# Seven products in place of eight in a feed-forward network's first down block, on one Trainium2 core

## The chip, the cores and the metric

The kernel runs on one core of a Trainium2 chip. The time is in device microseconds (us) of one execution. A core has TensorE (matrix products; the profile calls it PE, and its weight loads PEld), VectorE (DVE), ScalarE (ACT), GpSimd (POOL), SyncE (SP, which here only issues DMA transfers) and 16 DMA engines. Each engine works through its own instructions in order and waits on semaphores for the others.

## The reference

One layer of a causal decoder with 256 positions of 1024 channels in float32: attention of two kinds with a gated merge, then a gated feed-forward network with a causal convolution of width 3, then a last norm. The change lies in the feed-forward network:

```python
def conv_ffn(h, w_up, conv_w, conv_b, w_down):
    u, gate = jnp.split(h @ w_up, 2, axis=-1)          # each 256 x 2816
    up = jnp.pad(u, ((0, 0), (CONV_WIDTH - 1, 0), (0, 0)))
    uc = conv_b
    for j in range(CONV_WIDTH):
        uc = uc + conv_w[j] * up[:, j:j + S]
    return (jax.nn.gelu(uc) * gate) @ w_down           # 2816 x 1024
...
x = x + conv_ffn(rmsnorm(x, g_ffn[l]), w_up[l], conv_w[l], conv_b[l], w_down[l])
return rmsnorm(x, g_final)
```

## The kernel before

Every float32 operand of a matrix product is split in two parts that TensorE takes at its faster float32r rate: a high part (a copy rounded to float32r) and a low part (the value less the high part). A product is then three: high x high, high x low and low x high. For the weights, ScalarE makes the high part (`split_hi`, L131, tile whi) and VectorE the low one (`split_lo`, L135, tile wlo).

The weights come in units of 128 x 2048 numbers (1 MB), each loaded by one DMA transfer on SP's queue into one of three `raw` buffers; whi and wlo have three buffers each, too. The list `units` is walked in order, and the loop body writes out by hand what each engine does around a unit: at the start of a step the low part of the next unit (`lo_of(i + 1)`) and the load five units ahead, then the unit's products, then the high part of the unit two ahead (`hi_of(i + 2)`), then the evacuation. A raw buffer is free for the load three units later once both parts are made.

The feed-forward network goes in 11 blocks of 256 of the 2816 hidden channels. Block j has an up unit u_j, a gate unit g_j and a down unit d_j, and a down unit comes two blocks late: the order is u0 g0 u1 g1 u2 g2 d0 u3 g3 d1 u4 g4 d2 and so on. NFIRST is the number of u0 in the list, so that units NFIRST + 4, 5, 7 and 8 are u2, g2, u3 and g3. After u_j VectorE scales the result (U, L599), ScalarE and VectorE convolve it (C, L603, L611); after g_j ScalarE applies the gelu (L617), and VectorE multiplies (M, L624). M is then split like a weight: ah on ScalarE (L634) and al on VectorE (L643, `post_g`, issued a unit later).

A down unit multiplies M (two halves t of the positions by two halves kt of the channels) with 256 x 1024 weights. One half of the output columns takes the plain form (`mm_down_part`, L662). For the other half, blocks 1 to 8 use a form of the 2 x 2 block product with seven products instead of eight (`mm_sums`, L676): it needs sums of the four pieces of M (L629, L631, L632, which widen ah and al from 512 to 1024 columns) and of the four pieces of the weights (`split_sums`: W, L172 to L174, and its parts Wh, L176, and Wl, L178). Block 0 and the last two use the plain form for both halves. With the three products of each split, a down unit in the plain form is 48 products of 128 x 256, one with the seven-product form 24 + 21 = 45. `FIRST_SUM = 1` is the first block of that form.

Of the kernel before, what the change touches and what calls it, by code (L numbers as in the profile page):

```python
# [11 lines left out]
F32 = mybir.dt.float32  # L12
F32R = mybir.dt.float32r
# [14 lines left out]
SHARED = {25: 1024, 26: 1024}  # L28
ORDER = np.arange(D).reshape(8, 4, 32).transpose(1, 0, 2).reshape(-1)
QUARTERS = ((0, 0, 512), (1, 0, 512), (0, 512, 256), (1, 512, 256), (1, 768, 256), (0, 768, 256))  # L30
FIRST_SUM = 1
EPS = 1e-6
BIG = 1e30
UW = 2240
# [62 lines left out]
def build(ctx, tc, a, out):  # L97
# [35 lines left out]
    def split_lo(u, c0=0, c1=None, eng=None):  # L133
        c1 = c1 or u.n
        (eng or V).tensor_sub(u.lo[:, u.o + c0:u.o + c1], u.raw[:, c0:c1], u.hi.bitcast(F32)[:, u.o + c0:u.o + c1])  # L135

    def split_range(u, c0, c1):
        split_hi(u, c0, c1)
        split_lo(u, c0, c1)

    def hi_of(i):
        if 2 <= i < len(units):
            if units[i].load is not None or units[i] is downs[NF - 1] and units[i].hi is not None:
                return
            split_tiles(units[i])
            split_hi(units[i], 0, 1792 if units[i] in downs[FIRST_SUM:NF - 2] else None)

    def lo_of(i):
        if 2 <= i < len(units):
            if i == 27:  # L150
                split_lo(units[i], 1024, 2048, P)
                return
            if i in SHARED:
                split_lo(units[i], 0, SHARED[i])
                split_lo(units[i], SHARED[i], 2048, P)
                return
            if i == NFIRST + 1:
                split_lo(units[i], 0, 1024)
                split_lo(units[i], 1024, 2048)
                return  # L160
            if units[i] in downs[FIRST_SUM:]:
                return
            if units[i].load is None:
                split_lo(units[i])
# [424 lines left out]
        units.append(Unit(2048, mm_out(c), ev_out(c)))  # L589


    ffn = {}

    def ev_u(j):
        def f(u):
# [24 lines left out]
    def ev_g(j):  # L620
        def f(u):
            f_ = ffn["pool"]
            M = f_.tile([128, 8, 128], F32, name="M", tag="M", bufs=2)
            V.tensor_tensor(out=M[:, 0:4].rearrange("p (c t) s -> p c (t s)", c=2), in0=u.p, in1=ffn["C", j],  # L624
                            op=OP.mult)
            n = 4
            if FIRST_SUM <= j < NF - 2:
                n = 8
                V.tensor_tensor(out=M[:, 4:6], in0=M[:, 0:4:3], in1=M[:, 1, None].to_broadcast([128, 2, 128]),  # L629
                                op=OP.subtract)  # L630
                V.tensor_tensor(out=M[:, 6], in0=M[:, 5], in1=M[:, 0], op=OP.add)  # L631
                V.tensor_sub(M[:, 7], M[:, 2], M[:, 6])  # L632
            h = f_.tile([128, 8, 128], F32R, name="ah", tag="ah", bufs=4)
            A.activation(h[:, :n], M[:, :n], AF.Copy)  # L634
            ffn["M", j] = M[:, :n], h
        return f

    def post_g(j):
        def f():
            M, h = ffn["M", j]  # L640
            n = M.shape[1]
            l = ffn["pool"].tile([128, 8, 128], F32R, name="al", tag="al", bufs=4)
            V.tensor_sub(l[:, :n], M, h.bitcast(F32)[:, :n])  # L643
            ffn["a", j] = (h, l)
        return f
# [22 lines left out]
    def mm_sums(u, j):  # L668

        wh, wl = [w[:, u.o + 1024:u.o + 1792].rearrange("p (b c) -> p b c", b=3) for w in (u.hi, u.lo)]  # L670
        sh, sl = [w.rearrange("p (b c) -> p b c", b=4) for w in (u.wh, u.wl)]
        h, l = ffn["a", j]
        for q, x, k in ((2, 2, 1), (1, 0, 0), (3, 7, 2), (6, 6, 6), (5, 5, 4), (7, 4, 5), (4, 3, 7)):
            yh, yl = (wh[:, k], wl[:, k]) if k < 4 else (sh[:, k - 4], sl[:, k - 4])
            for n, (w, a_) in enumerate(((yh, h), (yh, l), (yl, h))):
                T.matmul(ffn["P"][q], a_[:, x], w, start=j == FIRST_SUM and n == 0 and q in (1, 5),  # L676
                         stop=j == NF - 3 and n == 2 and q in (1, 5, 6, 7), skip_group_check=True)

    def mm_down(j):
# [534 lines left out]
            nc.sync.dma_start(X[32 * j:32 * j + 32, :, b * 256:b * 256 + 256],  # L1214
                              Y[32 * b:32 * b + 32, :, j * 256:j * 256 + 256])

    post = []
    for i, u in enumerate(units):
        if i == FIRST_ITEM:
            rt["identr"] = att.tile([128, 128], F32R, name="identr")  # L1220
            A.activation(rt["identr"], ident, AF.Copy)
        if i == 9:
            cmp_sum()
        for it in batches.get(i - 1, []):
            it.fin()
        if i == FIRST_ITEM + 6:
            dil_tiles()
        for it in at(i):
            if isinstance(it, Dil):
                it.split()  # L1230
        for it in at(i - 3):
            it.te()
        if i == 11:
            cmp_kv_ev()
        for it in at(i - 1):
            it.sm()
        if i > 2 and i != 6:
            lo_of(i + 1)
        if i == 10:
            cmp_gelu()  # L1240
        for it in at(i - 1):
            it.sm2()
        for it in at(i - 1):
            it.send("MA" if isinstance(it, Cmp) else {20: "KH", 21: "KL"}.get(i, "MB%d" % (i % 2)))
        if u in downs[3:7]:
            spread(downs.index(u) - 3)
        load_to(i + LA)
        if i == 14:
            nc.sync.dma_start(xT, a["xT"])
        if i == 3:  # L1250
            hi_of(5)
            mixer_tiles()
            u1.evac(u1)
        if i == 4:
            split_keys()
        if i == 14:

            ob = att.tile([128, 4, S], F32R, name="ob", tag="qa")
            OB.update(h=ob[:, 0:2], l=ob[:, 2:4])
        if i in (23, 24):  # L1260
            for c in range(2):
                m = ML[i - 23, c]
                A.activation(m, m, AF.Sigmoid)
        if i == NFIRST:
            st.close()
            ffn["pool"] = ctx.enter_context(tc.tile_pool(name="ffn", bufs=1))
            gf = ffn["pool"].tile([128, D], F32, name="gf")
            nc.scalar.dma_start(gf, bass.AP(tensor=a["g_final"].tensor, offset=a["g_final"].offset,
                                            ap=[[0, 128], [1, D]]))
            X = ffn["pool"].tile([128, 2, D], F32, name="X")  # L1270
            sq = ffn["pool"].tile([128, 512], F32, name="sq")
            Y = ffn["pool"].tile([128, 2, D], F32, name="Y")
        if 24 <= i <= 25:
            hi_of(i + 2)
        if i in (3, 24, NFIRST + 2):
            rt["kick"] = "own"
        u.mm(u)
        if i == 2:
            split_tiles(units[3])
            for c in (0, 1024):  # L1280
                split_hi(units[3], c, c + 1024)
        if not 24 <= i <= 26 and i > 1 and i != 3:
            hi_of(i + 2)
        if i == 5:
            lo_of(7)
        if units[min(i + 2, len(units) - 1)] in downs[FIRST_SUM:NF - 2]:
            split_sums(units[i + 2])
        if units[min(i + 2, len(units) - 1)] is downs[NF - 2]:
            split_lo(units[i + 2])
        if i == 2:  # L1290
            lo_of(3)
            row_scale()
            u0.evac(u0)
            ev_cmp2()
        if i == NFIRST + 1:
            rt["R2"] = rows_of(rt["rs2"], "R2", "o")
            units[NFIRST].evac(units[NFIRST])
        if post:
            post.pop()()
        if u.pre:  # L1300
            u.pre(u)
        if i + 3 == len(units) - 1:
            hi_of(i + 3)
        if u.evac and i not in (0, 1, NFIRST):
            u.evac(u)
        if i + 3 == len(units) - 1:
            split_lo(units[i + 3])
        if i == 4:
            tables_pool4()
        if i in (6, 7):  # L1310
            q_parts(i - 6)
        if i == 7:
            gates_of()
        if u in downs[2:6]:
            turn(downs.index(u) - 2)
        if u.pre:
            post.append(post_g(len([q for q in units[:i] if q.pre])))
        first = [it for it in at(i) if isinstance(it, Nsa) or isinstance(it, Dil) and it.t]
        for it in first:
            it.qk()  # L1320
        if i == 11:
            at(i)[-1].by_keys()
        for it in at(i - 2):
            it.tr()
        for it in at(i):
            if it not in first:
                it.qk()
        for it in batches.get(i, []):
            it.pv()
        if i == 9:  # L1330
            cmp_fold()
        if i == 10:
            cmp_kv()
# [79 lines left out]
```

## Time and profile before

| what | value |
|---|---|
| median of 3 runs | 384.53 us (383.98 to 384.89) |
| the profiled execution: its time | 384.13 us |
| its span, first to last instruction | 382.2 us |
| granted TensorE clock, mean | 0.998 |
| busy: TensorE, VectorE, ScalarE, GpSimd | 374.9, 313.4, 225.1, 34.9 us |

The span is what the trace covers; some 1.9 us of the execution lie around it. A busy share is an average over stages. In rows of the timeline the first number is the start in us from the span's start, the second the length in us, then engine, line, operation, output <- inputs with shapes, and, in brackets, idle time of that engine just before and what ended it. The chain is followed back from the last instruction: each step to what released it, or to the instruction before it on its engine.

### The profile page before, as it was taken

Reading aid. Unit: us, or ns where it says so; the run is one execution under the profiler, and the core shown is the slowest. Engines: PE = TensorE matmul, PEld = TensorE weight load, DVE = VectorE, ACT = ScalarE, POOL = GpSimd, SP = SyncE. Lnnn points to the kernel's source line nnn. Section 1 sums busy time; section 2 is a strip of 40 time slices with the busy share of each in tenths; the row PEclk is TensorE's granted clock in tenths of the full one; section 3 lists DMA queues with packets and bytes.
Section 4 is the critical chain, followed back from the end, with each engine's and each line's share of the span. In section 5 each row is a group of like instructions: output and inputs, shape, how many; then the busy total and the mean of one; then the engine's idle time right before and its main releaser. Section 6 shows DMA issues by size and latency. Waiting matters only on the chain.

```text
span 382.2 us, 8160 instructions
## 1 busy us (share of the span) xinstructions
PE 374.9 (98%) x3393; PEld 369.3 (97%) x3393; DVE 313.4 (82%) x541; ACT 225.1 (59%) x315; POOL 34.9 (9%) x62
## 2 busy tenths in 40 slices
PE   8999999999999999999999999999999999999993
PEld 6999999999999999999999999999999999999993
DVE  5959699994996876468887799997998989889874
ACT  5966636875985745745634756554574455745613
POOL 4011400001000000250333000000000000000011
PEclk9999999999999999999999999999999999999999
DMA  8999354468454656463547355845658476585002
GB/s 274 423 391 345 138 218 168 166 237 332 172 201 150 233 222 224 151 220 101 202 149 290 126 211 199 322 146 187 219 177 294 148 239 229 156 304 202 21 0 110
DMA packets 14996, 79.30 MB, mean 207 GB/s; under 512 B 1776, under 2 KB 3312, under 8 KB 7280
## 3 DMA queue, kind: packets, MB, share of 16 engines
q1 hardware_dynamic: 14528, 77.94, 56.3%
q10 hardware_dynamic: 432, 0.85, 0.7%
q8 instruction: 26, 0.43, 0.4%
q14 instruction: 10, 0.08, 0.1%
HBM read 71.05 MB, written 1.05 MB: 189 GB/s over the span
## 4 chain that ended last, share of the span: by engine, by line
PE 96%; DMA 1%; DVE 0%; ACT 0%; issue 0%; SPq 0%; POOLq 0%; POOL 0%; ACTq 0%
PE ps_d L206 36%; PE ps_d L211 18%; PE ps_o L206 5%; PE ps_s L662 5%; PE ps_t L662 4%; PE ps_d L309 3%; PE ps_o L676 3%; PE ps_o L211 3%; PE ps_d L366 2%; PE ps_t L206 2%; PE ps_t L909 2%; DMA first<-in_first_dram 1%; PE ps_o L978 1%; PE ps_t L676 1%; PE ps_o L564 1%; PE ps_o L1099 1%
## 5 line engine op out<-in xcount | busy, mean ns | idle before, releaser
L135 DVE TENSOR_TENSOR wlo<-raw,whi 128x2048 fp32r<-128x2048 f32 (+3 forms) x62 | 132.5, 2140 | 4.5 <-ACT whi L131 4.5
L206 PE MATMUL ps_d<-hTh,whi 128*128 128x256 f32 x512 | 119.0, 278 | 0.0
L206 PE MATMUL ps_d<-hTl,whi 128*128 128x256 f32 x512 | 117.9, 276 | 0.0
L131 ACT ACTIVATE whi<-raw 128x2048 fp32r<-128x2048 f32 (+3 forms) x62 | 112.7, 1828 | 7.3 <-DMA raw<-in_wts_dram 3.1
L206 PEld LDWEIGHTS ps_d<-hTh,whi 128*128 128x128 f32 x512 | 96.1, 188 | 0.9 <-issue 0.7
L206 PEld LDWEIGHTS ps_d<-hTl,whi 128*128 128x128 f32 x512 | 96.1, 188 | 0.0
L211 PE MATMUL ps_d<-hTh,wlo 128*128 128x256 f32 x512 | 63.3, 276 | 0.0
L211 PEld LDWEIGHTS ps_d<-hTh,wlo 128*128 128x128 f32 x512 | 60.5, 188 | 0.0
L634 ACT ACTIVATE ah<-M 128x1024 fp32r<-128x1024 f32 (+1 forms) x11 | 10.4, 946 | 23.1 <-DVE M L632 19.9
L603 ACT ACTIVATE C<-U,small 128x256 f32<-128x256 f32 x22 | 12.0, 595 | 17.7 <-DVE U L599 17.7
L176 ACT ACTIVATE Wh<-W 128x1024 fp32r<-128x1024 f32 x8 | 8.5, 1064 | 22.4 <-DVE W L174 22.4
L611 DVE SCALAR_TENSOR_TENSOR C<-U,small,C 128x256 f32<-128x256 f32 x44 | 18.6, 480 | 2.1 <-ACT C L603 2.1
L946 ACT ACTIVATE E<-E,ast 128x256 f32<-128x256 f32 (+1 forms) x32 | 14.1, 450 | 9.6 <-DVE ast L941 7.7
L1357 POOL TENSOR_TENSOR tiny<-cst,tiny 128x1 f32<-128x1 f32 x2 | 0.5, 228 | 163.0 <-ACT sq L1356 163.0
L624 DVE TENSOR_TENSOR M<-ps_d,C 128x512 f32<-128x512 f32 x10 | 6.9, 690 | 10.0 <-PE ps_d L211 8.5
L135 POOL TENSOR_TENSOR wlo<-raw,whi 128x1024 fp32r<-128x1024 f32 x3 | 7.8, 2598 | 71.3 <-ACT whi L131 71.3
L643 DVE TENSOR_TENSOR al<-M,ah 128x1024 fp32r<-128x1024 f32 (+1 forms) x11 | 11.8, 1072 | 0.0
L206 PE MATMUL ps_d<-whi,hTh 128*128 128x256 f32 x48 | 11.3, 282 | 0.0
L206 PE MATMUL ps_d<-whi,hTl 128*128 128x256 f32 x48 | 11.1, 277 | 0.0
L206 PE MATMUL ps_o<-mixh,whi 128*128 128x256 f32 x48 | 11.0, 276 | 0.0
L206 PE MATMUL ps_o<-mixl,whi 128*128 128x256 f32 x48 | 11.0, 276 | 0.0
L381 DVE TENSOR_TENSOR ML<-ps_d,R 128x512 f32<-128x512 f32 x8 | 5.5, 690 | 6.3 <-PE ps_d L211 6.3
(314 smaller groups left out, 787.2 us busy)
## 6 DMA issues: line engine op xcount, KB each, us to landing
raw<-in_wts_dram SPq DMA_DIRECT2D x59, 1024.0 KB, 5.1
Er<-E SPq DMA_DIRECT2D x6, 512.0 KB, 3.2
first<-in_first_dram SPq DMA_DIRECT2D x7, 384.0 KB, 6.6
Er<-E SPq DMA_DIRECT2D x6, 384.0 KB, 2.9
raw<-in_wts_dram SPq DMA_DIRECT2D x2, 560.0 KB, 8.7
xn<-in_xn_dram SPq DMA_DIRECT2D x2, 512.0 KB, 8.9
w1k<-in_wts_dram SPq DMA_DIRECT2D x2, 512.0 KB, 7.8
w1v<-in_wts_dram SPq DMA_DIRECT2D x2, 512.0 KB, 7.6
```

The source lines that it names most:

```text
L131: A.activation(u.hi[:, u.o + c0:u.o + c1], u.raw[:, c0:c1], AF.Copy)
L135: (eng or V).tensor_sub(u.lo[:, u.o + c0:u.o + c1], u.raw[:, c0:c1], u.hi.bitcast(F32)[:, u.o + c0:u.o + c1])
L206: T.matmul(po, l, r, start=start and bank not in banks, stop=False, skip_group_check=True)
L211: T.matmul(po, l, r, start=False, stop=stop and n == len(ks) - 1, skip_group_check=True)
L309: T.matmul(u.p[:, i], l[:, kt, i * 128:i * 128 + 128], r[:, kt], start=kt == 0 and i == 0 and q == 0, stop=kt == 7 and q == 2, skip_group_ ...
L603: A.activation(C[:, c], U[:, c, 2:], AF.Identity, scale=CW(2, t), bias=CB[:, t:t + 1])
L611: V.scalar_tensor_tensor(C[:, c], U[:, c, w:w + S], CW(w, t), C[:, c], op0=OP.mult, op1=OP.add)
L634: A.activation(h[:, :n], M[:, :n], AF.Copy)
L643: V.tensor_sub(l[:, :n], M, h.bitcast(F32)[:, :n])
L662: T.matmul(ffn["y"][t][ch][:, b:b + 256] if own is None else own, x[:, 2 * kt + t], quarter(w, kt, ch, b), start=j == (0 if own is None el ...
L676: T.matmul(ffn["P"][q], a_[:, x], w, start=j == FIRST_SUM and n == 0 and q in (1, 5), stop=j == NF - 3 and n == 2 and q in (1, 5, 6, 7), s ...
L946: A.activation(self.E[:, i], self.E[:, i], AF.Exp, bias=mn[:, i:i + 1], scale=-1.0, accum_out=dn[:, i:i + 1])
```

## The change

Three things change. First, block 0's down unit takes the seven-product form, too (FIRST_SUM is 0). Second, the sums of M and the making of ah, now in a function `sums`, come later for the first blocks: those of block 0 after g1, of block 1 after g2, of block 2 after d0; from block 3 on they stand after their own g unit as before. Third, for u2, g2, u3 and g3 the second half of the low part (columns 1024 to 2048) is no longer made by VectorE: ScalarE writes the negated, rounded raw weights into it, and a DMA transfer from GpSimd's queue adds the raw weights to it in place.

```diff
-FIRST_SUM = 1
+FIRST_SUM = 0
+NEXT, LATE = {0: (), 1: (0,), 2: (1,)}, (2,)
+ADDED = (4, 5, 7, 8)
...
+    def negate_and_add(u, c0, c1):
+        lo = u.lo[:, u.o + c0:u.o + c1]
+        A.activation(lo, u.raw[:, c0:c1], AF.Copy, scale=-1.0)
+        P.dma_start(out=lo.bitcast(F32), in_=u.raw[:, c0:c1], accum_op=OP.add)
...
             split_hi(units[i], 0, 1792 if units[i] in downs[FIRST_SUM:NF - 2] else None)
+            if i - NFIRST in ADDED:
+                negate_and_add(units[i], 1024, 2048)
...
+            if i - NFIRST in ADDED:
+                split_lo(units[i], 0, 1024)
+                return
...
-            n = 4
-            if FIRST_SUM <= j < NF - 2:
-                n = 8
...
-            h = f_.tile([128, 8, 128], F32R, name="ah", tag="ah", bufs=4)
-            A.activation(h[:, :n], M[:, :n], AF.Copy)
-            ffn["M", j] = M[:, :n], h
+            for k in NEXT.get(j, (j,)):
+                sums(k)
...
+    def sums(j):
+        M, n = ffn["M", j], 4
+        if j < NF - 2:
+            n = 8
...
+        h = ffn["pool"].tile([128, 8, 128], F32R, name="ah", tag="ah", bufs=4)
+        A.activation(h[:, :n], M[:, :n], AF.Copy)
+        ffn["a", j] = h, None
+        post.append(post_g(j, M[:, :n], h))
...
-                T.matmul(ffn["P"][q], a_[:, x], w, start=j == FIRST_SUM and n == 0 and q in (1, 5),
+                T.matmul(ffn["P"][q], a_[:, x], w, start=j == 0 and n == 0 and q in (1, 2, 4, 5),
...
-        if u.pre:
-            post.append(post_g(len([q for q in units[:i] if q.pre])))
+        if u is downs[0]:
+            for k in LATE:
+                sums(k)
```

The order of the instructions shows where this lands. Names in the rows: whi and wlo are the weights' parts, C, M, U, W, ah and al as above. On ScalarE, from the gelu of block 0 to that of block 1 and what follows, before:

```order
L617 ACTIVATE C<-C 128x512 [waits DVE_49]
L634 ACTIVATE ah<-M 128x512 [waits DVE_49]
L131 ACTIVATE whi<-raw 128x2048 [waits DMAHW7_49,PE_49,Activation_49]
L603 ACTIVATE C<-U,small 128x256 [waits DVE_49]
L603 ACTIVATE C<-U,small 128x256
L131 ACTIVATE whi<-raw 128x2048 [waits DMAHW0_49,PE_49,Activation_49]
L617 ACTIVATE C<-C 128x512 [waits DVE_49]
L634 ACTIVATE ah<-M 128x1024 [waits DVE_49]
```

And after, at the same place:

```order
L629 ACTIVATE C<-C 128x512 [waits DVE_49]
L133 ACTIVATE whi<-raw 128x2048 [waits DMAHW7_49,PE_49,Activation_49]
L141 ACTIVATE wlo<-raw 128x1024 [waits PE_49]
L615 ACTIVATE C<-U,small 128x256 [waits DVE_49]
L615 ACTIVATE C<-U,small 128x256
L133 ACTIVATE whi<-raw 128x2048 [waits DMAHW0_49,PE_49,Activation_49]
L141 ACTIVATE wlo<-raw 128x1024 [waits PE_49]
L629 ACTIVATE C<-C 128x512 [waits DVE_49]
L652 ACTIVATE ah<-M 128x1024 [waits DVE_49]
```

The narrow ah of block 0 is gone from its place (the last row is now block 0's wide one, one block later), and a negated copy stands behind each high part, ahead of the next gelu.

On VectorE, from the low part of u2 (unit NFIRST + 4) to U of block 2, before:

```order
L135 TENSOR_TENSOR wlo<-raw,whi 128x2048 [waits DMAHW7_49]
L624 TENSOR_TENSOR M<-ps_o,C 128x512 [waits PE_49,Activation_49]
L629 TENSOR_TENSOR M<-M 128x256 [waits DVE_49]
L631 TENSOR_TENSOR M<-M 128x128 [waits DVE_49]
L632 TENSOR_TENSOR M<-M 128x128 [waits DVE_49]
L135 TENSOR_TENSOR wlo<-raw,whi 128x2048 [waits DMAHW0_49]
L643 TENSOR_TENSOR al<-M,ah 128x1024 [waits Activation_49]
```

And after:

```order
L137 TENSOR_TENSOR wlo<-raw,whi 128x1024 [waits DMAHW7_49]
L637 TENSOR_TENSOR M<-ps_o,C 128x512 [waits PE_49,Activation_49]
L647 TENSOR_TENSOR M<-M 128x256
L649 TENSOR_TENSOR M<-M 128x128 [waits DVE_49]
L650 TENSOR_TENSOR M<-M 128x128 [waits DVE_49]
L137 TENSOR_TENSOR wlo<-raw,whi 128x1024 [waits DMAHW0_49]
L184 TENSOR_TENSOR W<-raw 128x512 [waits DMAHW1_49]
L185 TENSOR_TENSOR W<-W,raw 128x256 [waits DVE_49]
L186 TENSOR_TENSOR W<-W,raw 128x256 [waits DVE_49]
L137 TENSOR_TENSOR wlo<-raw,whi 128x1792 [waits Activation_49]
L660 TENSOR_TENSOR al<-M,ah 128x1024
```

The low parts of u2 and g2 are half as long, the sums after M are block 0's instead of block 1's, and d0's weight sums and low part now stand here, ahead of al.

On GpSimd (POOL), after the norm's last step (L244, now L256), where before nothing came until the kernel's end:

```order
L256 TENSOR_TENSOR tiny<-tiny,cst 128x2 [waits Activation_49]
L142 DMA wlo<-raw 128x1024 [waits DMAHW7_49,DVE_49,Activation_49]
L142 DMA wlo<-raw 128x1024 [waits DMAHW0_49,DVE_49,Activation_49]
L142 DMA wlo<-raw 128x1024 [waits DMASW0_49,DMAHW2_49,DVE_49,Activation_49]
L142 DMA wlo<-raw 128x1024 [waits DMASW1_49,DMAHW3_49,DVE_49,Activation_49]
L1374 TENSOR_TENSOR tiny<-cst,tiny 128x1 [waits Activation_49]
```

The four accumulating transfers are new on this queue; each waits for ScalarE's negated copy. In u2, g2, u3 and g3 the fifth low-part product on TensorE waits for the transfer, the first one for VectorE as before.

More of the change, by code (lines that the diff above doesn't have):

```diff
@@ L589, in build @@
         units.append(Unit(2048, mm_out(c), ev_out(c)))
-    ffn = {}
+    ffn, post = {}, []
     def ev_u(j):
@@ L623, in f, with post_g @@
             M = f_.tile([128, 8, 128], F32, name="M", tag="M", bufs=2)
+            ffn["M", j] = M
             V.tensor_tensor(out=M[:, 0:4].rearrange("p (c t) s -> p c (t s)", c=2), in0=u.p, in1=ffn["C", j],
                             op=OP.mult)
-            n = 4
-            if FIRST_SUM <= j < NF - 2:
-                n = 8
[L629 to L632, printed above, removed]
-            h = f_.tile([128, 8, 128], F32R, name="ah", tag="ah", bufs=4)
-            A.activation(h[:, :n], M[:, :n], AF.Copy)
-            ffn["M", j] = M[:, :n], h
-        return f
-    def post_g(j):
+            for k in NEXT.get(j, (j,)):
+                sums(k)
+        return f
+    def sums(j):
+        M, n = ffn["M", j], 4
+        if j < NF - 2:
+            n = 8
+            V.tensor_tensor(out=M[:, 4:6], in0=M[:, 0:4:3], in1=M[:, 1, None].to_broadcast([128, 2, 128]),
+                            op=OP.subtract)
+            V.tensor_tensor(out=M[:, 6], in0=M[:, 5], in1=M[:, 0], op=OP.add)
+            V.tensor_sub(M[:, 7], M[:, 2], M[:, 6])
+        h = ffn["pool"].tile([128, 8, 128], F32R, name="ah", tag="ah", bufs=4)
+        A.activation(h[:, :n], M[:, :n], AF.Copy)
+        ffn["a", j] = h, None
+        post.append(post_g(j, M[:, :n], h))
+    def post_g(j, M, h):
         def f():
-            M, h = ffn["M", j]
             n = M.shape[1]
@@ L1215, in spread @@
                               Y[32 * b:32 * b + 32, :, j * 256:j * 256 + 256])
-    post = []
     for i, u in enumerate(units):
```

## The prediction

> **What bounds the kernel now.** I read the page's busy times first, then the chain that ended last, then the chain, the ScalarE rows and the VectorE rows of 205 to 255 us, where the changed instructions stand, and last the DMA issues.
>
> ```profile
> PE 374.9 (98%) x3393; PEld 369.3 (97%) x3393; DVE 313.4 (82%) x541; ACT 225.1 (59%) x315; POOL 34.9 (9%) x62
> PE 96%; DMA 1%; DVE 0%; ACT 0%; issue 0%; SPq 0%; POOLq 0%; POOL 0%; ACTq 0%
> ```
>
> TensorE is busy for 374.9 of 382.2 us and holds 96% of the chain: what another engine does counts only once it makes TensorE wait. The chain around the first down product, in order of time (start, length, what):
>
> ```profile
> 221.09 3.63 PE ps_d L206 x32
> ...
> 226.53 3.63 PE ps_d L206 x32
> ...
> 230.15 1.81 PE ps_d L211 x16
> 231.97 0.23 PE ps_s L662 x2
> ...
> 237.18 0.23 PE ps_s L662 x2
> 237.41 3.63 PE ps_d L206 x32
> ...
> 242.85 3.63 PE ps_d L206 x32
> 246.47 1.81 PE ps_d L211 x16
> 248.29 0.45 PE ps_s L662 x4
> ...
> 252.03 1.02 PE ps_o L676 x9
> 253.05 0.34 PE ps_s L676 x3
> 253.39 0.68 PE ps_d L206 x6
> ```
>
> Each piece starts where the last ended, so TensorE has no gap here. d0 (48 products) runs from 231.97 to 237.41, 5.44 us; d1 (24 products of L662 and 21 of L676) from 248.29 to 253.39, 5.10 us. u2, g2, u3 and g3 start at 221.09, 226.53, 237.41 and 242.85; each multiplies the high part for 3.63 us (L206) and the low part for 1.81 us (L211).
>
> **The change part by part.** *The seven products in d0.* d0 becomes what d1 is: 45 products for 48, so 5.44 - 5.10 = 0.34 us less on the path. Everything after d0 starts 0.34 us sooner if nothing is late. This is the only term that shortens the chain; the rest has to stay hidden.
>
> *What ScalarE does for it.* Its rows before:
>
> ```profile
> 213.75 0.63 ACT L617 ACTIVATE C<-C 128x512 f32<-128x512 f32 x1
> 215.14 0.63 ACT L634 ACTIVATE ah<-M 128x512 fp32r<-128x512 f32 x1 [0.76 <-DVE M L624]
> 215.68 1.91 ACT L131 ACTIVATE whi<-raw 128x2048 fp32r<-128x2048 f32 x1
> 218.55 1.10 ACT L603 ACTIVATE C<-U,small 128x256 f32<-128x256 f32 x2 [0.97 <-DVE U L599]
> 219.55 1.91 ACT L131 ACTIVATE whi<-raw 128x2048 fp32r<-128x2048 f32 x1
> 221.36 0.62 ACT L617 ACTIVATE C<-C 128x512 f32<-128x512 f32 x1
> ...
> 238.36 1.71 ACT L131 ACTIVATE whi<-raw 128x1792 fp32r<-128x1792 f32 x1 [0.22 <-DMA raw<-in_wts_dram]
> ...
> 242.34 1.07 ACT L176 ACTIVATE Wh<-W 128x1024 fp32r<-128x1024 f32 x1 [2.27 <-DVE W L174]
> ```
>
> Added: four negated copies of 128x1024 (1.07 each by the Wh row), a Wh for d0 (1.07), and ah of block 0 at 1024 for 512 (0.43 more); d0's high part is 0.20 shorter. Together 5.6 us on an engine that is 59% busy by the page. *What VectorE does.* Its rows before:
>
> ```profile
> 215.02 2.28 DVE L135 TENSOR_TENSOR wlo<-raw,whi 128x2048 fp32r<-128x2048 f32 x1
> 217.22 0.68 DVE L643 TENSOR_TENSOR al<-M,ah 128x512 fp32r<-128x512 f32 x1
> 217.83 0.68 DVE L599 TENSOR_TENSOR U<-ps_o,R 128x512 f32<-128x512 f32 x1
> ...
> 223.08 0.69 DVE L624 TENSOR_TENSOR M<-ps_o,C 128x512 f32<-128x512 f32 x1
> 223.80 0.42 DVE L629 TENSOR_TENSOR M<-M 128x256 f32<-128x256 f32 x1
> ...
> 224.79 2.29 DVE L135 TENSOR_TENSOR wlo<-raw,whi 128x2048 fp32r<-128x2048 f32 x1
> ...
> 240.70 0.68 DVE L172 TENSOR_TENSOR W<-raw 128x512 f32<-128x512 f32 x1
> ...
> 242.22 2.02 DVE L135 TENSOR_TENSOR wlo<-raw,whi 128x1792 fp32r<-128x1792 f32 x1
> 244.17 0.68 DVE L599 TENSOR_TENSOR U<-ps_d,R 128x512 f32<-128x512 f32 x1
> ...
> 245.90 1.67 DVE L611 SCALAR_TENSOR_TENSOR C<-U,small,C 128x256 f32<-128x256 f32 x4
> ...
> 252.32 1.22 DVE L643 TENSOR_TENSOR al<-M,ah 128x1024 fp32r<-128x1024 f32 x1
> 253.45 2.28 DVE L135 TENSOR_TENSOR wlo<-raw,whi 128x2048 fp32r<-128x2048 f32 x1
> ```
>
> Start to start, a low part takes 2.20 us (215.02 to 217.22), one of 1024 takes 1.13 (252.32 to 253.45), the three W sums 1.52 (240.70 to 242.22), the d low part 1.95 (242.22 to 244.17) and the three M sums 0.99 (223.80 to 224.79). Added for d0: W sums 1.52, Wl 1.13, M sums of block 0 0.99, a longer al 0.52, less 0.25 for the shorter low part: 3.9. Removed: four times 2.20 - 1.13 = 4.3. VectorE's total barely falls (0.4 us); what changes is the order.
>
> *Who is late next.* I laid the new order out by hand with these lengths, from 214.38, where the row at 213.75 ends. The high part of u2 no longer waits behind ah: it ends at 216.2, its negated copy at 217.2. U of block 1 starts at 217.2 (no al ahead), C ends on ScalarE at 218.9, then the high part of g2 (220.7) and its negated copy (221.7). Only then comes the gelu (222.3), so M of block 1 ends at 223.0 (before 223.8), M sums of block 0 at 224.0, ah at 225.1, d0's high part at 226.7, d0's low part 228.7, al of block 0 229.9, U of block 2 230.5, its C on ScalarE 231.5, the high part of u3 233.3, its negated copy 234.3, gelu 234.9, M and the sums of block 1 236.7, ah 237.7, the high part of g3 239.5, its negated copy 240.5.
>
> TensorE asks for al of block 0 after 8 products of d0, at 231.97 + 0.91 = 232.9, where it is 3.0 us old. The halves that VectorE still makes are done by 221.5, 225.3, 237.9 and 241.1, wanted (3.63 us into each unit; u3 and g3 0.34 earlier) at 224.7, 230.2, 240.7 and 246.1. Later, the low part of u4 ends at 254.4 and is wanted at 253.39 - 0.34 + 3.63 = 256.7: 2.3 us, the narrowest of VectorE's own.
>
> *The accumulating transfers.* The fifth product of the low part waits for them, 4 x 0.113 = 0.45 us later than the first. From the end of the negated copy to that product there are 225.2 - 217.2 = 8.0 us for u2, 230.6 - 221.7 = 8.9 for g2, 241.2 - 234.3 = 6.9 for u3 and 246.6 - 240.5 = 6.1 for g3. No accumulating transfer is in this trace. The nearest rows (KB each, median us from issue to landing):
>
> ```profile
> raw<-in_wts_dram SPq DMA_DIRECT2D x59, 1024.0 KB, 5.1
> Er<-E SPq DMA_DIRECT2D x6, 512.0 KB, 3.2
> ...
> xn<-in_xn_dram SPq DMA_DIRECT2D x2, 512.0 KB, 8.9
> ```
>
> Low end: 3.2 us, the same 512 KB from SBUF to SBUF. High end: 8.9, the same size queued behind other loads. I take 5.1: the transfer reads its 512 KB and also the 512 KB it adds to, the bytes of one weight load. At 5.1 nothing waits; g3's lands 1.0 us early. The wait of TensorE would be about D - 6.1 for a landing time of D: 2.8 us at 8.9, so the sum lies between -0.34 and +2.5 us. Issuing them costs POOL alone, whose queue holds nothing else here. Nor does the held raw buffer matter at 5.1: u4's weights reuse u3's buffer, freed at 239.4 in place of 237.4, and land 5.1 later at 244.5, when ScalarE wants them at 247.9; g4's follow on SP's queue from 245.6 to 250.7, wanted at 253.1.
>
> Sum: -0.34 us against the profiled execution's 384.13 (span 382.2 and 1.9 around it), so 383.8 there. That execution lies 0.40 under the median of the runs, 384.53; for the median I forecast 384.2. A measurement of this kernel can tell about 0.2%, 0.77 us, from no change, so this counts as the same.
>
> **The rivals.** *The transfers land late (slower).* Place: the fifth low-part product of g3, then of u3. It costs the whole gain at D = 6.1 + 0.34 = 6.4 and +0.77 at 7.2; at 8.0 it gives 384.5 + 1.6 = 386.1. For it: the loads of raw, 5.1 us each, run all through, and g3's transfer is issued (240.5) while u4's load (239.4 to 244.5) runs. Against: the Er row's 3.2.
>
> *VectorE keeps POOL from issuing (slower).* Two rows show the two engines in each other's way:
>
> ```profile
> L135 POOL TENSOR_TENSOR wlo<-raw,whi 128x1024 fp32r<-128x1024 f32 x3 | 7.8, 2598 | 71.3 <-ACT whi L131 71.3
> L231 DVE SCALAR_TENSOR_TENSOR hTl<-xT,small,hTh x8: 473/850/1516, 184.3 to 201.0; 128x256 fp32r<-128x256 f32 x8
> ```
>
> The second runs from 473 to 1516 ns; the slow ones stand beside POOL's sums of squares (L579, L581). If an issue on POOL has to wait until VectorE pauses, then u2's, g2's and u3's go out at once (VectorE idles around 218, 222 and 234), but g3's falls into a low part and the W sums of d1, 239.9 to 242.5: 2.0 us later, landing at 247.6 for 246.6, a wait of 1.0 and a sum of +0.7, 385.2. Against it: POOL's part of a transfer is not arithmetic on SBUF, and no row here shows it. The Trainium skill's SBUF — State Buffer, SBUF: two separate sides, states such a rule: a transfer issued from GpSimd stalls while VectorE runs an operation in a two-port mode, since its descriptors can't be written. By that rule alone the sum would be +0.7; the section on who interferes with whom adds that a tensor_tensor operation, which VectorE's rows here are, takes only the read side; so by that page in full it stays at -0.34.
>
> *VectorE itself is late.* Were its chain 2.3 us longer than laid out, u4's low part would stop TensorE; at 3.3 us the sum is +0.7, 385.2. Against: VectorE's rows repeat within 0.01 us, and it idles until each of ScalarE's results, not by its own load.
>
> *More than 0.34 comes back (faster).* Nothing on the chain near d0 waits, so I see no place for another 0.43 us.
>
> **How the numbers follow.** Forecast, -0.34 with at most a small wait: 0.62. Transfers late by more than 1.1 us: 0.17, at 385.3 to 387. POOL held up by VectorE: 0.07; VectorE late: 0.06, both near 385.2. Faster by over 0.77 us: 0.08, by something not seen. The range: runs spread from 383.98 to 384.89, so the forecast's low is 383.7; upward it takes the late transfers to D = 8.0, 386.2, and leaves the rest. Same gets the forecast and half of the 0.13 near +0.7: 0.68; slower 0.24; faster 0.08.
>
> **What would show it.** d0 at 5.10 us with 21 products of L693, which is L676 now; four issues on POOL with landing times under 6.1 us; no wait of a low-part product in u2 to g3 or u4; al of block 0 some 3 us early. Wrong, if TensorE waits for a transfer there, if a landing time is over 7 us, or if something at the start or end of the kernel grew with a POOL queue in use.

## The result: slower by 1.2%, in two groups of executions

| kernel | median us | all executions, us |
|---|---|---|
| before | 384.31 | 383.98 to 384.89 (6) |
| changed | 388.71 | 386.48, 386.49, 386.93, 390.48, 390.77, 392.20 |

The ratio is 1.0119 (1.0089 to 1.0149). A ratio leaves out executions that lie over 1.5% above the fastest of their kernel; medians and lists hold them. The median lies in a gap: three executions stand 2.2 to 2.6 us above the kernel before, three 6.2 to 7.9. The profiled execution took 386.49 us (span 384.6), of the lower group. Its page:

```profile
PE 375.6 (98%) x3390; PEld 369.8 (96%) x3390; DVE 313.2 (81%) x548; ACT 230.1 (60%) x320; POOL 38.4 (10%) x66
q1 hardware_dynamic: 14528, 77.94, 56.2%
q0 software_dynamic: 576, 2.10, 2.8%
PE 87%; DMA 4%; ACT 3%; DVE 3%; issue 2%; POOLq 0%; POOL 0%; ACTq 0%
```

TensorE has three products fewer, yet a new DMA queue, q0, moves 2.1 MB, and DMA, ScalarE and VectorE now hold 10% of the chain. TensorE's own waits (us in total, times, longest) name the cause:

```profile
PE ps_d L223 <- DMA wlo<-raw: 1.6, 2, 1.3
```

Its timeline around u2 (last bracket: idle time ahead and what ended it):

```profile
221.33 0.28 PE L218 MATMUL ps_d<-hTh,whi 128*128 128x256 f32 x1
...
224.96 0.62 PE L223 MATMUL ps_d<-hTh,wlo 128*128 128x256 f32 x4
226.85 1.65 PE L223 MATMUL ps_d<-hTh,wlo 128*128 128x256 f32 x12 [1.28 <-DMA wlo<-raw]
228.34 0.28 PE L218 MATMUL ps_d<-hTh,whi 128*128 128x256 f32 x1
```

The fifth low-part product of u2 waits for the accumulating transfer. g2's first product comes at 228.34; 48 products after 221.33, at 5.44 us, it would be 226.77: 1.6 us lost. The second wait is g3's. The chain after it, again:

```profile
241.38 0.96 ACT wlo L141
242.34 0.28 issue
242.62 6.27 DMA wlo<-raw
...
248.94 1.63 PE ps_d L223 x12
...
255.66 3.63 PE ps_d L218 x32
```

u4 starts at 255.66, before at 253.39: 2.27 us later. The stretch began 0.41 late (the copy R at 210.53, before 210.12; the loads at the start differ from execution to execution), the three products give 0.34 back, and so 2.2 us are waits: 1.6 at u2, some 0.6 to 0.7 at g3. The span is 2.4 longer, so from u4 on nothing is lost in this execution. Where the other group's further 4 us go is not in it.

The issue of the four transfers in GpSimd's timeline:

```profile
217.86 1.10 POOL L142 DMA_DIRECT2D wlo<-raw  x1 [9.04 <-DVE U L610]
222.51 0.86 POOL L142 DMA_DIRECT2D wlo<-raw  x1 [3.55 <-ACT wlo L141]
236.54 0.86 POOL L142 DMA_DIRECT2D wlo<-raw  x1 [13.17 <-ACT wlo L141]
242.62 0.86 POOL L142 DMA_DIRECT2D wlo<-raw  x1 [5.22 <-ACT wlo L141]
```

And their times to landing, in the DMA issues of a window around each (us last; d0's load stands in the first window):

```profile
raw<-in_wts_dram SPq DMA_DIRECT2D x1, 1024.0 KB, 6.6
wlo<-raw POOLq DMA_DIRECT2D x1, 512.0 KB, 8.9
wlo<-raw POOLq DMA_DIRECT2D x1, 512.0 KB, 6.8
wlo<-raw POOLq DMA_DIRECT2D x1, 512.0 KB, 4.7
wlo<-raw POOLq DMA_DIRECT2D x1, 512.0 KB, 6.3
```

u2's is issued 0.1 us after d0's weight load (217.77) and takes 8.9 us; the load beside it takes 6.6. From 217.9 to 226.9 the DMA engines are 90% busy at 205 GB/s in the changed kernel (the last two columns):

```profile
217.90:226.90 9.00, 7.72 (x69) 7.52 (x67) 7.33 (x14) 6.80 (x7) 1.92 (x2) 1.00 0.90 205
```

And in the kernel before, in the same stretch, 61% at 218 GB/s:

```profile
217.90:226.90 9.00, 9.00 (x82) 9.00 (x81) 8.22 (x13) 5.42 (x6) 0.00 (x0) 1.00 0.61 218
```

The engines are busier and move less, by the bytes that the profile counts.

### The profile page after: what moved, and what is told of

It is laid out like the page before. It is cut to its first block, busy times and chain, and to the rows that moved or that the text cites. A ratio compares the mean times of both kernels' runs of the same rounds, so it can differ in the third digit from the quotient of the medians.

```text
span 384.6 us, 8185 instructions
## 1 busy us (share of the span) xinstructions
PE 375.6 (98%) x3390; PEld 369.8 (96%) x3390; DVE 313.2 (81%) x548; ACT 230.1 (60%) x320; POOL 38.4 (10%) x66
## 3 DMA queue, kind: packets, MB, share of 16 engines
q1 hardware_dynamic: 14528, 77.94, 56.2%
## 4 chain that ended last, share of the span: by engine, by line
PE 87%; DMA 4%; ACT 3%; DVE 3%; issue 2%; POOLq 0%; POOL 0%; ACTq 0%
PE ps_d L218 32%; PE ps_d L223 16%; PE ps_s L679 4%; PE ps_t L679 4%; PE ps_o L218 3%; PE ps_d L378 3%; PE ps_d L321 3%; PE ps_o L693 3%; PE ps_t L218 2%; PE ps_t L926 2%; PE ps_o L223 2%; DMA raw<-in_wts_dram 2%; DMA wlo<-raw 2%; PE ps_o L995 1%; PE ps_t L693 1%
## 5 line engine op out<-in xcount | busy, mean ns | idle before, releaser
L137 DVE TENSOR_TENSOR wlo<-raw,whi 128x2048 fp32r<-128x2048 f32 (+3 forms) x62 | 128.0, 2066 | 4.9 <-ACT whi L133 4.8
L188 ACT ACTIVATE Wh<-W 128x1024 fp32r<-128x1024 f32 x9 | 9.6, 1063 | 20.1 <-DVE W L186 20.1
L190 DVE TENSOR_TENSOR Wl<-W,Wh 128x1024 fp32r<-128x1024 f32 x9 | 10.9, 1214 | 0.0
```

## The experiments

Theory 1: the accumulating transfers cost, by the time that they take to land. Theory 2: the new order on VectorE costs. Four kernels tell them apart; 1 and 2 below are parts of the change, the third is the changed kernel again.

**1. Seven products and later sums, no transfers.**

```diff
-ADDED = (4, 5, 7, 8)
+ADDED = ()
```

> The changed kernel without the negated copies and the accumulating transfers: VectorE makes all of the four low parts again; the seven products in block 0 and the later sums stay. Theory 1 (the transfers' landing, 4.7 to 8.9 us, is what costs): all of the loss goes and the 3 products saved are left, 384.3 - 0.3 = 384.0 us, executions again within about 0.5 us of each other. Theory 2 (the new order, VectorE's added work for block 0, is what costs): VectorE now has 4.3 us more in this stretch, so it gets worse than the changed kernel's 386.5 to 392 us, with TensorE waiting for VectorE's low parts or al.

Measured: 383.60 us median (12 executions, 383.28 to 384.30), ratio 0.9986 (0.9976 to 0.9996): faster than before by 0.14%, 0.5 us against the 0.34 of the three products. TensorE waits for nothing in the feed-forward network. With the later sums VectorE did not need the relief: theory 2 falls, and this is the version that beats both kernels.

**2. The transfers alone**, on the kernel before (FIRST_SUM = 1, old sums, with `negate_and_add` for u2, g2, u3, g3):

```diff
+ADDED = (4, 5, 7, 8)
...
+            if i - NFIRST in ADDED:
+                negate_and_add(units[i], 1024, 2048)
...
+            if i - NFIRST in ADDED:
+                split_lo(units[i], 0, 1024)
+                return
```

> The kernel before with the negated copies and accumulating transfers for u2, g2, u3 and g3 alone; eight products in block 0 and the sums where they were. Theory 1: the same loss as in the changed kernel, plus the 0.34 us that the seven products saved: 386.8 us and more, executions spread over some us. Theory 2: VectorE has 4.3 us less to do, no loss: 384.3 us.

Measured: 385.47 us, ratio 1.0044 (1.0019 to 1.0069); eight of ten executions at 384.4 to 386.8, two at 389.5 and 390.7. The transfers lose time on their own. It is less than expected in the lower group: in this order ScalarE's negated copy of g3 comes 2.8 us sooner (issue at 239.80), and only u2's transfer is late, by 0.3 us in the profiled execution. It is issued 1.5 us after d0's load there, not 0.1, and lands after 6.2 us, not 8.9.

**3. The changed kernel again**, twice, for more profiles.

> The changed kernel once more, unaltered, for a second profile: six executions lay at 386.5 to 386.9 and at 390.5 to 392.2 us, with nothing between. Theory 1: the landing times differ between executions; an execution over 390 shows one or more transfers landing 4 us later than the 4.7 to 8.9 us seen, or a raw load held by one. Rival: the extra 4 us lie elsewhere (the start, the end, the granted clock 0.991 to 0.997), and the four landing times are as in the first profile.

> The changed kernel once more, for a profile: two profiles so far were executions of 386.5 and 387.0 us. If this one is over 389, theory 1 wants a transfer or a load held by one to land some 4 us later than in those; the rival wants the same landing times and the 4 us elsewhere.

Measured: 386.98, 385.67, 391.41 and 387.69 us, then one of 391.44. That last is of the upper group. Its transfers land as before (8.5, 6.4, 4.4 and 6.3 us), and TensorE's waits are no longer (1.3 us in all): theory 1 in the form expected is wrong for the upper group. The chain of this execution shows what is different, ahead of the same chain of the kernel before:

```profile
226.01 1.68 PE ps_d L223 x12
227.69 3.77 PE ps_d L218 x32
...
255.94 3.77 PE ps_d L218 x32
...
361.23 3.77 PE ps_d L218 x32
```

```profile
253.39 3.63 PE ps_d L206 x32
...
354.71 3.63 PE ps_d L206 x32
```

From the wait at u2 on, 32 products take 3.77 us, not 3.63: 117.8 ns each, not 113.4, to the end. From u4's start to g10's it is 105.3 us in place of 101.3, and with the rest at the same rate some 4.7 us: about the distance of the groups. The 30 us between u2's wait and u4 add some 1.1 (both are estimates from the two rates). The granted clock is 0.997 over the span, as in the profiled execution of the lower group, and 1.00 in both between 228 and 325 us, wherever it was read, so it isn't the clock. It is a second pace of TensorE's stream of products. That this kernel's other executions over 389 us owe their time to it, too, is inferred from their times: they were not profiled.

**4. GpSimd's subtraction instead.**

```diff
-        A.activation(lo, u.raw[:, c0:c1], AF.Copy, scale=-1.0)
-        P.dma_start(out=lo.bitcast(F32), in_=u.raw[:, c0:c1], accum_op=OP.add)
+        P.tensor_sub(lo, u.raw[:, c0:c1], u.hi.bitcast(F32)[:, u.o + c0:u.o + c1])
```

> The changed kernel with the second halves of the four low parts made by GpSimd's subtraction (as it does for three units earlier, 2.4 to 3.0 us each) instead of ScalarE's negated copy and a transfer. Theory 1: ready 3 us after the high part, 5 us or more ahead of TensorE's need; raw buffers are not held; 384.0 us. Rival (POOL and VectorE stop each other where both read two operands, as in the row of hTl that goes from 473 to 1516 ns): VectorE loses up to 2.6 us at each of four places against 2.3 us of spare, so 385 to 390 us.

Measured: 385.42 us, ratio 1.0028 (1.0016 to 1.0041), nine executions within 1.1 us. The rival holds. VectorE's sums of M next to a subtraction on GpSimd (timeline, rows of VectorE, then of GpSimd):

```profile
223.06 2.02 DVE L646 TENSOR_TENSOR M<-M 128x256 f32<-128x256 f32 x1
241.70 2.47 DVE L649 TENSOR_TENSOR M<-M 128x128 f32<-128x128 f32 x1
221.29 3.51 POOL L141 TENSOR_TENSOR wlo<-raw,whi 128x1024 fp32r<-128x1024 f32 x1 [1.36 <-ACT whi L133]
241.63 2.40 POOL L141 TENSOR_TENSOR wlo<-raw,whi 128x1024 fp32r<-128x1024 f32 x1 [3.92 <-ACT whi L133]
```

They take 2.02 and 2.47 us where the same operations took 0.41 and 0.29 in the changed kernel; each ends soon after GpSimd's (225.08 and 224.80, 244.17 and 244.03). VectorE's delay eats its 2.3 us of spare, and TensorE waits 0.5 us for u4's low part, after 0.2 for its high part.

**5. Why the transfers are slow: plain copies in their place.**

```diff
-        P.dma_start(out=lo.bitcast(F32), in_=u.raw[:, c0:c1], accum_op=OP.add)
+        P.dma_start(out=lo.bitcast(F32), in_=u.raw[:, c0:c1])
```

> The changed kernel with four plain copies on the same queue in place of the accumulating transfers (the addition of the negated part is left out). Theory 1a (the addition is what makes them long: the destination is read too): a plain copy of 512 KB lands in about 3.5 to 4.5 us (3.2 for the copy of E on SP's queue), takes about half of the DMA engines' time of the 2.6 us that an accumulating one takes, no product waits, 384.0 us. Theory 1b (GpSimd's queue is what makes them long): landing times stay at 5 to 9 us and the loss stays, 386.5 us and more.

Measured: 384.03 us, ratio 0.9996 (0.9986 to 1.0005), all ten executions between 383.4 and 384.6. Landing times 6.8, 3.5, 3.7 and 4.0 us, and on the page the queue takes 1.3% of the DMA engines' span for the same 2.1 MB:

```profile
q0 software_dynamic: 576, 2.10, 1.3%
wlo<-raw POOLq DMA_DIRECT2D x4, 512.0 KB, 3.8
```

2.8% of 384.6 us is 2.7 us of all 16 engines for each accumulating transfer, 1.3% of 382.3 is 1.2 for a plain one: the addition about doubles the work (theory 1a). The queue itself is not slow; only the copy beside d0's load is (6.8).

**6. Each pair alone.**

```diff
-ADDED = (4, 5, 7, 8)
+ADDED = (4, 5)
```

```diff
-ADDED = (4, 5, 7, 8)
+ADDED = (7, 8)
```

> The changed kernel with the transfers for u2 and g2 alone; VectorE makes u3's and g3's low parts. Theory 1: u2's transfer still runs beside d0's load and g2's transfer and lands near 8.9 us after its issue, TensorE waits 1.3 to 1.5 us for it: 384.0 + 1.4 = 385.4 us. If instead the loss came from the second pair, 384.0 us.

> The changed kernel with the transfers for u3 and g3 alone; VectorE makes u2's and g2's low parts. Theory 1: u2's wait of 1.4 us goes, u3's load no longer waits for u2's transfer and comes 1.3 us sooner; g3's transfer (6.3 us for 6.1) costs 0 to 1.2 us: 384.0 to 385.2 us.

Measured: the first pair 385.63 us, ratio 1.0037 (1.0018 to 1.0055), four of five executions at 385.2 to 386.0 and one at 391.8; u2's transfer took 9.0 us beside d0's load and TensorE waited 1.3 us, as expected. The second pair 390.03, ratio 1.0142 (1.0095 to 1.0189): 386.9, 389.5, 390.6 and 391.2. In the profiled one, of 391.23, TensorE waits once, at g3, and the pace changes there:

```profile
248.46 1.68 PE L223 MATMUL ps_d<-hTh,wlo 128*128 128x256 f32 x12 [1.64 <-DMA wlo<-raw]
```

That wait is 1.6 us, not the 0 to 1.2 expected: nothing had delayed TensorE at u2, so it asked sooner. So the slower pace can start at u2's wait (experiment 3) and at g3's alone.

**7. Transfers of half the size.**

```diff
-                negate_and_add(units[i], 1024, 2048)
+                negate_and_add(units[i], 1536, 2048)
...
-                split_lo(units[i], 0, 1024)
+                split_lo(units[i], 0, 1536)
```

> The changed kernel with transfers of 512 columns instead of 1024 (VectorE makes 1536 of each of the four low parts). Half of the added bytes, about 1.3 us less landing time each: u2's lands at 7 to 7.7 us, inside its 7.5 to 8, g3's at 5 for 6.1; no product waits or one by under 0.3 us: 384.0 us. If a wait is what sets TensorE's slower pace, no execution lies at 389 us or over.

Measured: 383.79 us, ratio 0.9985 (0.9972 to 0.9998), ten executions between 383.2 and 384.6. u2's transfer landed after 7.3 us, the others after 4.0, 3.2 and 4.4. No product waits, and none of the ten is in the upper group: transfers do no harm as long as TensorE does not wait for them. They do no good either: without any the ratio was 0.9986.

**8. The pace: more small products, or one fewer.** The kernel has a product of 64 columns ahead of u1 and two earlier units (`kick`). One kernel adds it at g2 and u4 of the changed kernel, one takes u1's away from the kernel before.

```diff
-        if i in (3, 24, NFIRST + 2):
+        if i in (3, 24, NFIRST + 2, NFIRST + 5, NFIRST + 10):
```

> The changed kernel with one more small product of 64 columns at the start of g2 and of u4, the first unit of plain form after each of the two waits, like the ones that the kernel already has ahead of u1 and two earlier units. If such a product sets the pace of those behind it back to 113.3 ns: no execution over 388 us, all at 386.5 to 387.2. If not: as the changed kernel, 386.5 to 387 and 390 to 392.

```diff
-        if i in (3, 24, NFIRST + 2):
+        if i in (3, 24):
```

> The kernel before without the small product of 64 columns ahead of u1. If the pace is set by how the first products after a wait fall: u1's first product follows a wait, and without the small one all of the feed-forward network may run at 117.7 ns or more a product, 163 us x 3.9% = 6 us longer, 390 us, with all of its low and high groups of 32 at 3.77 us or more. If the small product does nothing: 384.3 us.

Measured: with the added ones 387.4, 391.3, 392.1 and 394.4 us, ratio 1.0158 (1.0098 to 1.0219): the long executions stay, so the expectation was wrong. The profiled one, of 387.42, shows the small products changing the pace both ways, with no wait at either. Behind the wait at u2 the products soon start 113 ns apart again; behind g2's small product, at 228.18, they start 118 ns apart; and u4's small product (L213) sets them back to 113, so that 16 products take 1.81 us, where the slower pace makes it 1.89:

```profile
256.59 0.03 PE ps_d L213
256.62 3.73 PE ps_d L218 x32
260.35 1.81 PE ps_d L223 x16
```

Without u1's 389.9 to 391.1 us in four executions, ratio 1.0161 (1.0142 to 1.0180), with every group of 32 at the slower pace from u1 to the end. The 390 us were expected, but not for this reason: the trace has no wait ahead of u1, in this kernel or in the kernel before. First without the small product, then before (L201 is the small product):

```profile
206.66 2.93 PE ps_d L309 x24
209.59 0.22 PE ps_o L251 x2
209.81 3.77 PE ps_o L206 x32
213.58 1.89 PE ps_o L211 x16
...
359.98 3.77 PE ps_d L206 x32
```

```profile
206.93 2.93 PE ps_d L309 x24
209.87 0.22 PE ps_o L251 x2
210.08 0.03 PE ps_o L201
210.12 3.72 PE ps_o L206 x32
213.83 1.81 PE ps_o L211 x16
```

In both kernels the 24 products ahead of u1 start 118 ns apart already, behind four products of one column (L238). The small product ends that in the kernel before; without it the slower pace goes on. (The first product of such a group is some 0.1 us longer, which is in the 2.93, the 3.72 and the 3.73.)

So the pace can change wherever the run of equal products is broken, by a wait or by products of another shape, and then holds. Which way it falls behind a wait in mid-unit was different from execution to execution; without u1's small product it was the same in all four, by their times.

**9. Waits that VectorE ends.**

```diff
+            if i == NFIRST + 4:
+                split_lo(units[i], 0, 1024)
+                for _ in range(4):
+                    split_lo(units[i], 1024, 2048)
+                return
```

> The kernel before, no transfers, where VectorE makes the second half of u2's low part four times over, so that the fifth low-part product of u2 waits for VectorE until 226.5, 1.3 us, where the changed kernel waits for the transfer. Theory A (any wait of TensorE here can leave it at 117.7 ns a product in place of 113.3 for the rest, by chance): executions at 385.7 us and some at 390 to 391. Theory B (only a wait that a transfer ends does it): all of them at 385.6 to 386.

> The kernel before with u2's fifth low-part product made to wait for VectorE, once more, since three of its five executions told little: 385.9, 386.7 and 387.1 us, none near 390, and the two others far off at a granted clock unlike that of any other run. Theory A (any wait can leave TensorE at the slower pace, by chance): of some ten executions three or four at 389.5 us or over, as with the transfers, 13 of 33. Theory B (the wait must be ended by a transfer): none, all at 385.6 to 387.1.

> The changed kernel without the transfers and with the sums of M after their own g unit, as before: the seven products in block 0 alone. By VectorE's rows laid out in this order u2's low part ends near 225.4 us and is wanted at 224.7, so TensorE waits some 0.7 us for VectorE: 384.0 + 0.7 = 384.7 us where the later sums without transfers gave 383.6. If the order of the sums does not matter: 383.6. On the pace: if any wait can leave TensorE at 117.7 ns a product, some executions lie at 389 us or over; if only a wait that a transfer ends does, none.

Measured: the repeated low part first gave 385.9, 386.7 and 387.1 us (ratio 1.0063, 1.0041 to 1.0085), then, on another chip, 388.2, 388.3, 391.8, 393.9 and 394.0 (1.0184, 1.0134 to 1.0234); the two of 388 fit neither group. Three more executions of this kernel, of 633 to 2152 us, two of them at granted clocks of 0.56 and 0.78, are left out and unexplained. The profiled execution of 391.75 has one wait, ended by VectorE, and the slower pace behind it:

```profile
226.66 1.68 PE L216 MATMUL ps_d<-hTh,wlo 128*128 128x256 f32 x12 [1.90 <-DVE wlo L135]
```

In its chain:

```profile
228.34 3.77 PE ps_d L211 x32
```

The seven products alone, with the sums where they were, took 384.68 us, ratio 1.0014 (1.0005 to 1.0023): eleven executions at 384.5 to 385.4, one at 390.9. TensorE waits for VectorE's low parts, 0.6 us in two waits. Theory A holds: the wait need not be a transfer's. And the later sums are worth some 1 us: each against the kernel before on its own chip, 0.5 us are gained with them and 0.3 lost without. They are what keeps the seven products free of waits.

## Why the prediction was wrong

**The seven products.** Right: d0's 45 products take 5.10 us (233.78 to 238.88), 0.34 less, and the waits and the pace behind them took that back; without the transfers 0.5 us were gained, 384.13 to 383.60 on the same chip.

**The order on ScalarE and VectorE.** The rows laid out held to about 0.5 us up to d0: u2's copy was done at 217.5 (laid out 217.2, with the 0.41 of this execution's late start), al of block 0 at 230.3 (229.9), ahead of its use. From u3 on they fell behind: its high part waited 1.28 us for its load, which had been held back until u2's transfer gave the raw buffer free:

```profile
226.94 6.34 DMA raw<-in_wts_dram
...
233.39 1.92 ACT L133 ACTIVATE whi<-raw 128x2048 fp32r<-128x2048 f32 x1 [1.28 <-DMA raw<-in_wts_dram]
```

I had worked that hold out for u4's load alone, at 5.1 us, and not for u3's.

**The landing time.** This term failed. I took D = 5.1 us, from the load with the same bytes; measured were 8.9, 6.8, 4.7 and 6.3. The estimate of the work was about right (2.7 us of the DMA engines; 56.2% of the span for q1's 77.94 MB makes 2.9 us for a load), but that row's 5.1 is the time of a load that mostly runs by itself. u2's transfer ran beside d0's load and then g2's transfer, three at once: 8.5 to 9.1 us in the profiles where it was issued 0.1 us behind the load. My rival named this sharing for g3 and not for u2, to which I gave 8.0 us of allowance, and overlooked that d0's load starts when VectorE ends g1's low part (row at 215.02, 217.3), the very time of u2's issue. The rival's rule, a wait of D - 6.1, is g3's; at u2 it is D - 8.0. The measured landing times make that 0.9 at u2 and 0.2 at g3, 1.1 in all, and 2.2 were lost: 1.6 at u2, 0.6 to 0.7 at g3. The sum had left out the 0.3 us from the copy's end to the issue and the 0.3 that the first products behind a wait lose, and g3's copy ended at 242.3, not 240.5. So the 2.8 that the rule gives at 8.9 comes near by luck: wrong transfer, wrong allowance. Late transfers had 0.17; their upper end, 387.0, which holds the lower group's 386.5 to 386.9, was worked out in the prediction, but its range stops at 386.2.

**POOL held up by VectorE.** It did not happen: each issue follows the negated copy by 0.3 us, g3's at 242.62 in the midst of VectorE's low part (241.74 to 242.96). The rule of the Trainium skill's SBUF — State Buffer, SBUF: two separate sides, is about VectorE's two-port operations, and none of its rows beside the four issues is one: they are tensor_tensor operations. The Trainium skill's section on who interferes with whom exempts descriptors written beside those, and these four issues agree. Where GpSimd computes on SBUF itself, experiment 4 shows the stop that the same section of the Trainium skill states for a VectorE operation with two inputs there beside a GpSimd operation that reads there.

**What no term held.** I took a wait to cost its length. Here the pace behind a wait could add some 5 us from g3's wait to the end and some 6 from u2's (estimates from the two rates over the 134 and 157 us that are left in the execution of 391.44). The kernel before never waits in this network from u1 on, so its trace has one pace there; its attention part, which I had passed over, has the other one, too:

```profile
53.61 3.85 PE ps_d L206 x32
57.46 1.89 PE ps_d L211 x16
...
60.66 3.69 PE ps_d L206 x32
64.35 1.81 PE ps_d L211 x16
```

The first 48 products run at the slower pace, with no wait ahead of them, and the next 48 at the faster. This costs the prediction more than the landing time does: the late transfers' 2.2 us explain the lower group, and the upper group's further 4 us and more are this pace, as far as the profiles show it.

## What to carry to other kernels

Relief for an engine that isn't the bound paid nothing here; first run the saving without the relief. To price a transfer, find what else is in flight when it is issued, and count an accumulating one as about twice the work of a copy. In a long stream of products that TensorE runs without a gap, a wait can cost more than its length: look at the length of a group of equal products before and behind it, and do the same wherever products of another shape stand between two groups.

## What the runs showed of the hardware that I had not expected

TensorE's stream of 128x256 products, each with its own weight load, had two paces in this network at the same granted clock: 113.4 and 117.8 ns a product. It changed where the run of equal products was broken, at a wait, whoever ended it, or at products of another shape without any wait, and then, settled within some six products, held until the next break, for up to 170 us (without u1's small product). Four profiles show the slower pace to the end: three from a wait on (the changed kernel again, the second pair, VectorE's wait), one from u1 on without a wait. Two show it for a while: with the added small products from g2 to u4, and with GpSimd's subtraction between its two waits, the second of which ended it. Kernels that keep u1's small product and have no wait behind it had no execution of the upper group (none of 32: 12 without transfers, 10 with plain copies, 10 with half the size; and none of the 77 of the kernel before, the longest of 385.75 us); those with a wait in mid-unit had, in 1 of 12 up to 3 of 4 executions (the repeated low part in none of three, then in three of five), but for GpSimd's subtraction, with waits of 0.7 us and none in nine. What decides the pace at a break is open: not the length of a wait alone, nor who ends it, and a small product set it back at u1 and u4 and brought the slower one at g2.
